# Accumulating transfers in DRAM in place of two additions on engines, in one step of an encoder layer

## The chip, the cores and the metric

The kernel runs on one core of a Trainium2 chip. The metric is the device time of one execution in microseconds; the kernel before takes 2776.52 us (median of three runs).

## What is computed

One layer of an encoder for two groups of requests that share the weights: a prompt of 2048 tokens and eight samples of 16 tokens, 17 tiles of 128 tokens in all. After a mixer (attention and a matrix memory) comes the part that matters here, a feed-forward net with a convolution and a norm on its output:

```python
def conv_ffn(h, buf, w_up, w_conv, b_conv, w_down):
    S = h.shape[1]
    u = h @ w_up
    ext = jnp.concatenate([buf.astype(u.dtype), u], axis=1)
    y = b_conv
    for j in range(CONV_W):
        y = y + ext[:, j:j + S] * w_conv[j]
    gate, up = jnp.split(y, 2, axis=-1)
    out = (jax.nn.gelu(gate, approximate=True) * up) @ w_down
    return out, ext[:, S:]
...
    ffn, new_buf = conv_ffn(rms_norm(x, norm_g[2]), conv_buf, w_up, w_conv, b_conv, w_down)
    x = x + rms_norm(ffn, norm_g[3])
```

The model width is 1024, the inner width 2816 (22 slices of 128, for gate and up each).

## The kernel before

The net works on three blocks of tokens: block 0 and block 1 with six tiles each, block 2 with four prompt tiles and the sample tile. Each block has an up projection and then a down projection. Everything is float32, made of three matmuls on split values: every weight and every activation is split into a high part (ACT, L1309) and a low part (DVE, L1310) before it is multiplied, in the helper `split`.

**Up projection.** A loop over the 22 slices f (I call one of its turns a round; `ORDERS` takes f and f + 11 in turn in blocks 1 and 2). A round makes the gate and the up slice by a scheme of seven half-size products, 7 x 12 = 84 matmuls, 384 wide in block 1 and 320 in block 2. DVE adds the products' results into two tiles, `uu` and `ug` (L1483, L1619, L1621, L1642); three such tiles are handed out in turn. `conv` lets GpSimd (POOL) copy two columns of the neighbouring block into the tile (L1494, L1497) and two columns out of it (L1499, L1498), then ACT (L1502, L1506) and DVE (L1503, L1504) do the convolution, and DVE multiplies gate and up into `g` (L1652, L1655). In block 1 that product stands in the tile `y`.

**Activation sums.** In blocks 1 and 2 the down projection is a product by seven as well. For that `store_a` keeps, per pair of slices k and k + 11, the parts A11, A12, A22 and four sums in DRAM (the tensors `ad`). In the pair's second round DVE makes S3, S1, S2 and S4 (L1595) into four of the pool's six spare tiles, and POOL stores them (L1597). S1 is A21 + A22, where A21 is the second part of the pair's first tile and A22 the second part of its second tile. In block 2 the sample tile's columns are stored on their own (L1577).

**Delayed norms.** The down projection leaves the un-normed output halves f0 and f1 of each tile of blocks 0 and 1 in DRAM, and `unfinished` keeps the tile's scale. While the next block's up projection runs, one unit per round (12 in block 1, 12 in block 2, from the fourth round on) finishes half a tile: SP loads f (L1427) and the residual x (L1428) from DRAM into two spare tiles, DVE scales f by the row's scale and the norm's weights (L1431), POOL adds x (L1432) and POOL issues the store of the result into the output (L1433). The loads and the scaling keep their written place among the other instructions of SP and DVE (`keep_in_program_order`); all else is ordered by a scheduler that plans with a model of the engines, so a change in one step can move others.

SP issues the loads of weights and activations, POOL the stores of this part. The transfers that one engine issues start in its order, and an instruction that waits holds up all that stands behind it on that engine.

Of the kernel before, what the change touches and what calls it, by code (L numbers as in the profile page):

```python
# [13 lines left out]
ALU = mybir.AluOpType  # L14
# [35 lines left out]
def hymba_step(ctx: ExitStack, tc: tile.TileContext, I: dict, O: dict):  # L50
    nc = tc.nc
# [17 lines left out]
    def spare_tile(name):  # L69
        return spare.tile([P, 512], F32, tag="k", name=name)  # L70

    def dt_(shape, name):
        return dram.tile(shape, F32, tag=name, name=name)
# [22 lines left out]
    def norm_row(i):  # L96
        t = const.tile([P, D], F32, tag="grow", name=f"norm_row{i}")
        nc.sync.dma_start(t, I["norm_g"][i:i + 1, :].broadcast_to([P, D]))
        return t


    def mm3(out, ah, al, bh, bl, start, stop, onto=False):
# [20 lines left out]
    ad = {(b, what): dt_([P, NK, 256 if b == 2 and what in ("A22", "S2", "S3") else 384], f"ad{b}_{what}")  # L123
          for b in FAST for what in ("A11", "A12", "A22", "S1", "S2", "S3", "S4")}
# [3 lines left out]
    x2d = [dt_([P, D], f"x2d{t}") for t in range(17)]  # L128
# [933 lines left out]
    def row(name):  # L1062
        return ffn.p3.tile([P, D], F32, tag="yq", name=name, bufs=4)
# [181 lines left out]
    for n_, (half, gi) in enumerate(seq):  # L1245
        wh, wl, _ = pend
# [154 lines left out]
    def out_rows(t):  # L1401
        return O["y_sample"] if t == SAMPLE else O["y_prompt"][t * P:(t + 1) * P, :]
# [20 lines left out]
    def later(t, rs):  # L1423

        def unit(half):
            v, x, c = spare_tile(f"f{half}{t}"), spare_tile(f"x{half}{t}"), half * 512
            tc.keep_in_program_order(nc.sync.dma_start(v, (f0d, f1d)[half][t]))  # L1427
            tc.keep_in_program_order(nc.sync.dma_start(x, x2d[t][:, c:c + 512]))  # L1428
            yield 0.0, 0.0
            tc.keep_in_program_order(  # L1430
                nc.vector.scalar_tensor_tensor(v, v, rs, g3[:, c:c + 512], op0=ALU.mult, op1=ALU.mult))  # L1431
            nc.gpsimd.tensor_tensor(v, v, x, op=ALU.add)  # L1432
            nc.gpsimd.dma_start(out_rows(t)[:, c:c + 512], v)  # L1433
            yield 0.0, 1.0

        return [unit(half) for half in range(2)]

    def delayed(units):

        for u in units:  # L1440
            next(u)
            yield
            next(u)

    ph.close()
    p4 = ffn.p4 = ctx.enter_context(tc.tile_pool(name="p4", bufs=1, side="right", reuse_waits="tile"))
# [3 lines left out]
    g3 = norm_row(3)  # L1450
# [15 lines left out]
    for b, tiles in enumerate(FBLOCKS):  # L1466
# [108 lines left out]
        def store_a(f, gt):  # L1575
            put = lambda what, k, src: nc.gpsimd.dma_start(ad[b, what][:, k, :], src)
            own = lambda what, k, src: nc.gpsimd.dma_start(ad[b, what][:, k, 256:384], src)  # L1577
            w = 256 if last else 384
            k = f % NK
            if f < NK:  # L1580
                put("A11", f, gt[:, 0:384])
                if last:
                    own("S1", k, gt[:, 256:384])
                held[f] = gt
                return
            put("A12", k, gt[:, 0:384])
            put("A22", k, gt[:, 384:384 + w])
            if last:
                own("S4", k, gt[:, 256:384])
            gt1 = held.pop(k)  # L1590
            a11, a21, a12, a22 = gt1[:, 0:w], gt1[:, 384:384 + w], gt[:, 0:w], gt[:, 384:384 + w]
            s3, s1, s2, s4 = [spare_tile(f"s{x}_{b}_{k}")[:, :w] for x in (3, 1, 2, 4)]
            for o, x, y, op in ((s3, a11, a21, ALU.subtract), (s1, a21, a22, ALU.add), (s2, a22, s3, ALU.subtract),
                                (s4, a12, s2, ALU.subtract)):
                nc.vector.tensor_tensor(o, x, y, op=op)  # L1595
            for what, src in (("S3", s3), ("S1", s1), ("S2", s2), ("S4", s4)):
                nc.gpsimd.dma_start(ad[b, what][:, k, 0:w], src)  # L1597

        done = delayed([u for t, rs in unfinished for u in later(t, rs)])
        unfinished = []  # L1600
        for fi, f in enumerate(ORDERS[b]):
            w = pend.pop(0)
# [11 lines left out]
            e, c = ec[:, 0:512], ec[:, 512:1024]  # L1614
# [10 lines left out]
            w = pend.pop(0)  # L1625
# [21 lines left out]
            gt = yg if fast and not last else row(f"g{nm}")  # L1647
# [9 lines left out]
            if fast:  # L1657
                store_a(f, gt)
            else:
                nc.gpsimd.dma_start(gd[b][f][:, :nt * P], gt[:, :nt * P])  # L1660
# [147 lines left out]
        for dh in range(2):  # L1808
# [59 lines left out]
            for j in order:  # L1868
                if dh == 0:
                    half, ssq = out[j]  # L1870
# [3 lines left out]
                else:  # L1874
                    half, ssq = out[j]
# [3 lines left out]
                    rs = p3.tile([P, 1], F32, tag=f"drs{j}", name=f"drs{tiles[j]}", bufs=2)  # L1879
# [104 lines left out]
```

## Time and profile before

| | us |
|---|---|
| median of three runs | 2776.52 |
| fastest and slowest of the three | 2768.33, 2780.66 |
| the profiled execution | 2780.55 |
| its span | 2778.8 |
| up projection of block 1 | about 1862 to 2165 of the span |
| up projection of block 2 | about 2352 to 2640 of the span |

PE is TensorE (PEld its weight loads), DVE VectorE, ACT ScalarE, POOL GpSimd, SP SyncE; a q behind a name means the engine's queue, which waits and issues. A row of instructions names line, engine, operation, output <- inputs and shape; behind the bar stand busy time, mean time of one in ns, and the idle time before them with what ended it. A row of a stretch gives its start and end, its length, then busy time and number of instructions per engine, PE's granted clock (1.00 is full), the share of time that the 16 DMA engines moved data, and GB/s. A row of transfers gives how many, KB each, and the median us from issue to landing.

### The profile page before, as it was taken

How to read it: one execution, taken by the hardware profiler on the slowest of the kernel's cores; microseconds unless marked ns; L12 is line 12 of the kernel's file. 1: busy time of each engine (PE TensorE's matmuls, PEld its weight loads, DVE VectorE, ACT ScalarE, POOL GpSimd, SP SyncE). 2: the span in 40 equal slices, each digit the busy share in tenths (PEclk: the TensorE clock that was granted, in tenths of full speed). 3: DMA queues.
4: the chain of work that ended last, by engine and by line, in shares of the span. 5: the costliest groups of instructions: out<-in, count | busy, mean ns of one | idle time of the engine just before them, and what ended most of it. 6: DMA issues, size and time to landing. Idle time of an engine off the chain costs nothing.

```text
span 2778.8 us, 47788 instructions
## 1 busy us (share of the span) xinstructions
PE 2700.5 (97%) x16422; PEld 2525.1 (91%) x16422; DVE 1971.7 (71%) x3637; ACT 1439.6 (52%) x2918; POOL 658.6 (24%) x1249
## 2 busy tenths in 40 slices
PE   7999999999999999999999999999999999999998
PEld 7899999998899998878999998789999778989976
DVE  5244455645546668766989987668998866999966
ACT  4355555634346666543555455445455665545554
POOL 1000010211100002335433322123442112555301
PEclk9999999999999999999999999999999999999999
DMA  5534355556564456345645559866775766777775
GB/s 182 157 116 139 105 164 168 163 152 211 156 184 141 136 169 196 107 163 195 230 153 188 167 183 329 301 224 198 225 225 170 250 223 231 216 236 231 233 268 183
DMA packets 322850, 532.52 MB, mean 192 GB/s; under 512 B 59650, under 2 KB 156638, under 8 KB 322478
## 3 DMA queue, kind: packets, MB, share of 16 engines
q1 hardware_dynamic: 251838, 400.11, 46.6%
q0 software_dynamic: 25840, 83.98, 7.9%
q10 hardware_dynamic: 44928, 45.37, 5.0%
q8 instruction: 129, 2.11, 0.3%
q14 instruction: 115, 0.94, 0.1%
HBM read 383.28 MB, written 149.18 MB: 192 GB/s over the span
## 4 chain that ended last, share of the span: by engine, by line
PE 49%; DVE 5%; DMA 3%; issue 2%; ACT 1%; POOL 1%; SPq 0%; DVEq 0%; POOLq 0%; ACTq 0%
PE uec L104 5%; PE uec L105 5%; PE uec L106 5%; PE dn L106 4%; PE dn L105 3%; PE dn L104 3%; PE ua L106 3%; PE ua L105 3%; PE ua L104 3%; PE wo L106 2%; PE wo L104 2%; PE wo L105 2%; PE dnm L105 1%; PE dnm L106 1%; PE dnm L104 1%
## 5 line engine op out<-in xcount | busy, mean ns | idle before, releaser
L104 PE MATMUL uec<-B,wuh 128*128 128x384 f32 (+1 forms) x720 | 237.8, 331 | 11.8 <-DVE uu L1642 10.7
L105 PE MATMUL uec<-B,wuh 128*128 128x384 f32 (+1 forms) x720 | 236.5, 328 | 0.0
L106 PE MATMUL uec<-B,wul 128*128 128x384 f32 (+1 forms) x720 | 234.8, 328 | 0.0
L1309 ACT CAST wuh<-wu 128x512 fp32r<-128x512 f32 x255 | 141.4, 618 | 112.4 <-PE uec L105 105.4
L1310 DVE TENSOR_TENSOR wul<-wu,wuh 128x512 fp32r<-128x512 f32 x255 | 170.4, 703 | 4.0 <-DMA x2d<-mx 2.8
L405 DVE CUSTOM_DVE_ANT_0 tmp<-s,nb 128x640 f32<-128x640 f32 (+4 forms) x128 | 94.4, 738 | 95.6 <-PE s L395 94.2
L104 PE MATMUL vo<-wi_h,hT 128*128 128x256 f32 x544 | 155.2, 285 | 0.8 <-DVE mt L211 0.6
L106 PE MATMUL vo<-wi_h,hT 128*128 128x256 f32 x544 | 155.6, 286 | 0.0
L105 PE MATMUL vo<-wi_l,hT 128*128 128x256 f32 x544 | 154.8, 285 | 0.0
L104 PEld LDWEIGHTS uec<-B,wuh 128*128 128x128 f32 x720 | 136.2, 189 | 15.3 <-DVE uu L1642 12.4
L104 PE MATMUL qk<-hT,wi_h 128*128 128x384 f32 (+1 forms) x384 | 130.3, 339 | 7.4 <-ACT qk_st L236 4.1
L105 PEld LDWEIGHTS uec<-B,wuh 128*128 128x128 f32 x720 | 136.4, 189 | 0.2
L106 PEld LDWEIGHTS uec<-B,wul 128*128 128x128 f32 x720 | 136.2, 189 | 0.0
L1506 ACT ACTIVATE y<-y 128x768 f32<-128x768 f32 (+1 forms) x66 | 53.8, 815 | 155.5 <-DVE y L1504 155.5
L418 DVE TENSOR_TENSOR ptl<-pt,pth 128x640 fp32r<-128x640 f32 (+4 forms) x128 | 93.7, 738 | 56.5 <-ACT pth L417 55.5
L406 ACT ACTIVATE tmp<-tmp,mn 128x640 f32<-128x640 f32 (+4 forms) x128 | 97.6, 762 | 64.2 <-DVE mn L405 62.4
L1310 DVE TENSOR_TENSOR wdl<-wdr,wdh 128x512 fp32r<-128x512 f32 x198 | 124.9, 686 | 7.0 <-ACT wdh L1309 6.8
L105 PE MATMUL qk<-hT,wi_h 128*128 128x384 f32 (+1 forms) x384 | 128.9, 336 | 0.0
L106 PE MATMUL qk<-hT,wi_l 128*128 128x384 f32 (+1 forms) x384 | 128.5, 335 | 0.0
L1310 DVE TENSOR_TENSOR al<-ar,ah 128x768 fp32r<-128x768 f32 (+2 forms) x94 | 71.1, 765 | 80.9 <-ACT ah L1309 80.7
L105 PE MATMUL qb<-hT,wi_h 128*128 128x384 f32 (+1 forms) x384 | 127.9, 333 | 0.0
L106 PE MATMUL qb<-hT,wi_l 128*128 128x384 f32 (+1 forms) x384 | 127.2, 331 | 0.0
(443 smaller groups left out, 9443.9 us busy)
## 6 DMA issues: line engine op xcount, KB each, us to landing
wu<-in_w_up SPq DMA_DIRECT2D x220, 256.0 KB, 4.4
wu<-wsd SPq DMA_DIRECT2D x176, 256.0 KB, 4.1
wdr<-in_w_down SPq DMA_DIRECT2D x110, 256.0 KB, 5.8
wi_raw<-in_w_in SPq DMA_DIRECT2D x52, 512.0 KB, 4.0
wsd<-ws POOLq DMA_DIRECT2D x88, 256.0 KB, 3.7
wdr<-wtd SPq DMA_DIRECT2D x88, 256.0 KB, 4.8
gr<-gd SPq DMA_DIRECT2D x39, 384.0 KB, 5.9
kraw<-kTd SPq DMA_DIRECT2D x112, 128.0 KB, 3.2
```

The lines of the kernel that those rows point to most:

```text
L104: nc.tensor.matmul(out, ah, bh, start=start, stop=False, skip_group_check=onto)
L105: nc.tensor.matmul(out, ah, bl, start=False, stop=False, skip_group_check=onto)
L106: nc.tensor.matmul(out, al, bh, start=False, stop=stop, skip_group_check=onto)
L405: nc.vector.tensor_tensor_reduce(o_, s_, b_, 1.0, 3e38, ALU.add, ALU.min, accum_out=mn)
L406: nc.scalar.activation(tmp[:, :n], tmp[:, :n], AF.Exp, bias=mn, scale=-1.0, accum_out=rsum[:, i % 4, hh:hh + 1])
L418: nc.vector.tensor_tensor(s.ptl[:, sl, qc], ptv, s.pth[:, sl, qc], op=ALU.subtract)
L1309: nc.scalar.copy(h, r)
L1310: nc.vector.tensor_tensor(l, r, h, op=ALU.subtract)
L1506: nc.scalar.activation(y[:, :ln], y[:, :ln], AF.Gelu_apprx_tanh)
```

## The change

A delayed unit no longer loads x and no longer adds it on POOL. Once DVE has scaled f, POOL issues a transfer that adds the tile onto x in DRAM, where x lies (`x2d`), and one that copies the sum from there to the output. In the code the copy of a unit is written one unit later, behind the next unit's accumulation. A unit takes one spare tile in place of two.

S1 is no longer made by DVE: POOL stores A21 as S1 in the pair's first round and adds A22 onto it in DRAM by an accumulating transfer in the second. A pair takes three spare tiles in place of four, and issues one transfer more.

```diff
@@ -1423,24 +1423,25 @@
     def later(t, rs):
 
         def unit(half):
-            v, x, c = spare_tile(f"f{half}{t}"), spare_tile(f"x{half}{t}"), half * 512
+            v, c = spare_tile(f"f{half}{t}"), slice(half * 512, half * 512 + 512)
             tc.keep_in_program_order(nc.sync.dma_start(v, (f0d, f1d)[half][t]))
-            tc.keep_in_program_order(nc.sync.dma_start(x, x2d[t][:, c:c + 512]))
             yield 0.0, 0.0
             tc.keep_in_program_order(
-                nc.vector.scalar_tensor_tensor(v, v, rs, g3[:, c:c + 512], op0=ALU.mult, op1=ALU.mult))
-            nc.gpsimd.tensor_tensor(v, v, x, op=ALU.add)
-            nc.gpsimd.dma_start(out_rows(t)[:, c:c + 512], v)
-            yield 0.0, 1.0
+                nc.vector.scalar_tensor_tensor(v, v, rs, g3[:, c], op0=ALU.mult, op1=ALU.mult))
+            nc.gpsimd.dma_start(x2d[t][:, c], v, accum_op=ALU.add)
+            yield 0.0, 0.7
+            nc.gpsimd.dma_start(out_rows(t)[:, c], x2d[t][:, c])
+            yield 0.0, 0.0
 
         return [unit(half) for half in range(2)]
 
     def delayed(units):
 
-        for u in units:
-            next(u)
+        for u, old in zip(units + [iter([])], [iter([])] + units):
+            next(u, None)
             yield
-            next(u)
+            next(u, None)
+            next(old, None)
 
     ph.close()
     p4 = ffn.p4 = ctx.enter_context(tc.tile_pool(name="p4", bufs=1, side="right", reuse_waits="tile"))
@@ -1579,21 +1580,22 @@
             k = f % NK
             if f < NK:
                 put("A11", f, gt[:, 0:384])
+                nc.gpsimd.dma_start(ad[b, "S1"][:, k, 0:w], gt[:, 384:384 + w])
                 if last:
                     own("S1", k, gt[:, 256:384])
                 held[f] = gt
                 return
             put("A12", k, gt[:, 0:384])
             put("A22", k, gt[:, 384:384 + w])
+            nc.gpsimd.dma_start(ad[b, "S1"][:, k, 0:w], gt[:, 384:384 + w], accum_op=ALU.add)
             if last:
                 own("S4", k, gt[:, 256:384])
             gt1 = held.pop(k)
             a11, a21, a12, a22 = gt1[:, 0:w], gt1[:, 384:384 + w], gt[:, 0:w], gt[:, 384:384 + w]
-            s3, s1, s2, s4 = [spare_tile(f"s{x}_{b}_{k}")[:, :w] for x in (3, 1, 2, 4)]
-            for o, x, y, op in ((s3, a11, a21, ALU.subtract), (s1, a21, a22, ALU.add), (s2, a22, s3, ALU.subtract),
-                                (s4, a12, s2, ALU.subtract)):
-                nc.vector.tensor_tensor(o, x, y, op=op)
-            for what, src in (("S3", s3), ("S1", s1), ("S2", s2), ("S4", s4)):
+            s3, s2, s4 = [spare_tile(f"s{x}_{b}_{k}")[:, :w] for x in (3, 2, 4)]
+            for o, x, y in ((s3, a11, a21), (s2, a22, s3), (s4, a12, s2)):
+                nc.vector.tensor_tensor(o, x, y, op=ALU.subtract)
+            for what, src in (("S3", s3), ("S2", s2), ("S4", s4)):
                 nc.gpsimd.dma_start(ad[b, what][:, k, 0:w], src)
 
         done = delayed([u for t, rs in unfinished for u in later(t, rs)])
```

The order on POOL around a unit, in block 2's up projection. Before, with `f_27653` the scaled half of a tile and `x_27654` its residual, `halo` and `sext` the columns kept between blocks, `uu` and `ug` the convolution's tiles:

```order
L1499 COPY halo<-ug_14_27734 128x2
L1498 COPY sext<-ug_14_27734 128x16
L1432 TENSOR_TENSOR f_27653<-f_27653,x_27654 128x512
L1433 DMA out_y_prompt<-f_27653 128x512
L1494 COPY uu_15_28059<-halo 128x2
L1497 COPY uu_15_28059<-sext 128x8x2
L1499 COPY halo<-ug_4_27911 128x2
L1498 COPY sext<-ug_4_27911 128x16
```

In the changed kernel the same place on POOL, where `x2d_288` is the residual's tile in DRAM (the lines of `conv` are one further on):

```order
L1500 COPY halo<-ug_14_27686 128x2
L1499 COPY sext<-ug_14_27686 128x16
L1431 DMA x2d_288<-f_27607 128x512
L1433 DMA out_y_prompt<-x2d_288 128x512
L1495 COPY uu_15_28006<-halo 128x2
L1498 COPY uu_15_28006<-sext 128x8x2
L1500 COPY halo<-ug_4_27859 128x2
L1499 COPY sext<-ug_4_27859 128x16
```

The scheduler put the copy to the output straight behind the accumulation that it waits for, ahead of the convolution's column copies. In block 2 six of the twelve units stand so; in the other six, two, four, one, two, four and two of the column copies come in between, 15 in all.

On DVE the rows of a pair's second round in block 2 (slices 2 and 13), before:

```order
L1642 TENSOR_TENSOR uu_3_27550<-x_2_3_27497,uec_3_27495 128x320
L1652 TENSOR_TENSOR g_13_27448<-y_13_0_27443,y_13_1_27435 128x2x256
L1655 TENSOR_TENSOR g_13_27448<-y_13_0_27443,y_13_1_27435 128x128
L1621 TENSOR_TENSOR x_2_14_27662<-x_2_14_27661,uec_14_27659 128x320
L1595 TENSOR_TENSOR s_2_2_27455<-g_2_27284,g_13_27448 128x256
L1595 TENSOR_TENSOR s_2_2_27456<-g_13_27448,s_2_2_27454 128x256
L1503 SCALAR_TENSOR_TENSOR y_3_1_27614<-uu_3_27550,wcv,y_3_1_27614 128x656
L1595 TENSOR_TENSOR s_2_2_27457<-g_13_27448,s_2_2_27456 128x256
```

and in the changed kernel:

```order
L1644 TENSOR_TENSOR uu_3_27503<-x_2_3_27450,uec_3_27448 128x320
L1654 TENSOR_TENSOR g_13_27405<-y_13_0_27400,y_13_1_27392 128x2x256
L1657 TENSOR_TENSOR g_13_27405<-y_13_0_27400,y_13_1_27392 128x128
L1623 TENSOR_TENSOR x_2_14_27614<-x_2_14_27613,uec_14_27611 128x320
L1597 TENSOR_TENSOR s_2_2_27413<-g_13_27405,s_2_2_27412 128x256
L1504 SCALAR_TENSOR_TENSOR y_3_1_27567<-uu_3_27503,wcv,y_3_1_27567 128x656
L1597 TENSOR_TENSOR s_2_2_27414<-g_13_27405,s_2_2_27413 128x256
```

The sum of the two tiles g_2 and g_13, which is S1, is gone; the rest of this piece stands in its old order.

## The prediction

> **What bounds the kernel now.** I read the page's first part, then busy times by stage, then what PE and DVE waited for in the one stage that loses time, then groups and single instructions there.
>
> ```profile
> PE 2700.5 (97%) x16422; PEld 2525.1 (91%) x16422; DVE 1971.7 (71%) x3637; ACT 1439.6 (52%) x2918; POOL 658.6 (24%) x1249
> ```
>
> PE is busy for 97% of the span, so at most 78 us could be won anywhere. The stages from the up projection of block 1 on, where the change acts:
>
> ```profile
> core 0: us, PE busy (x) PEld busy (x) DVE busy (x) ACT busy (x) POOL busy (x), PEclk, DMA share, GB/s
> 1862.00:2165.00 303.00, 302.28 (x1735) 301.96 (x1735) 275.12 (x406) 154.25 (x252) 112.05 (x179) 1.00 0.63 201
> 2165.00:2360.00 195.00, 191.76 (x900) 157.65 (x899) 135.21 (x210) 118.80 (x222) 29.90 (x59) 1.00 0.73 239
> 2360.00:2400.00 40.00, 40.00 (x275) 40.00 (x274) 37.22 (x77) 24.14 (x42) 17.56 (x38) 1.00 0.64 201
> 2400.00:2560.00 160.00, 149.88 (x988) 148.09 (x987) 151.59 (x296) 80.52 (x139) 94.57 (x171) 0.97 0.74 236
> 2560.00:2620.00 60.00, 60.00 (x411) 60.00 (x410) 55.91 (x118) 33.92 (x59) 26.40 (x62) 1.00 0.60 191
> ```
>
> Row one is block 1's up projection, with 12 delayed units: PE idles 0.7 of 303 us, so nothing is to be won there. Rows three to five are block 2's. Before its delayed units (2360 to 2400) and behind them (2560 to 2620) PE never idles. While the 12 units run (2400 to 2560), it does. At the pace of the fifth row (411 matmuls in 60 us, 6.85 per us) the 988 matmuls would take 144.2 us; they took 160. **The stretch loses 15.8 us**: 10.1 us of idle PE (160 less 149.88), and 5.7 us of slow matmuls. I call one value of f a round, 84 matmuls (7 products of 12): 11.8 rounds of 12.26 us at full pace.
>
> ```profile
> PE uec L104 <- DVE uu L1642: 9.7, 4, 4.2
> ```
>
> PE's idle time there is four waits for DVE. DVE was busy 151.59 us over work that PE needs 144.2 us for: 105%. Behind the units it is 55.91 of 60, 93%. So in this stretch alone DVE sets the pace. The longest wait, on the chain:
>
> ```profile
> 2463.80 6.03 DMA f<-f1d
> ...
> 2475.80 0.64 PE uec L104
> 2476.43 0.27 PE uec L105
> ```
>
> After it matmuls start every 0.27 us in place of 0.146 (60 over 411): the slow part.
>
> **The change part by part.** POOL's add of the residual goes, 24 times. Its price is paid by DVE as well:
>
> ```profile
> 2525.10 1.93 DVE L1503 SCALAR_TENSOR_TENSOR y<-ug,wcv,y 128x656 f32<-128x656 f32 x1
> ...
> 2527.35 0.89 DVE L1504 SCALAR_TENSOR_TENSOR y<-ug,wcv,y 128x656 f32<-128x656 f32 x1
> ```
> ```profile
> 2524.66 1.67 POOL L1432 TENSOR_TENSOR f<-f,x 128x512 f32<-128x512 f32 x1 [0.69 <-DVE f L1431]
> ```
>
> The DVE instruction that lies under the add takes 1.93 us, its like a moment later 0.89. For all adds, the groups of DVE with the units (2400 to 2556):
>
> ```profile
> L1310 DVE TENSOR_TENSOR wul<-wu,wuh 128x512 fp32r<-128x512 f32 x52 | 38.4, 768 | 0.0
> L1310 DVE TENSOR_TENSOR wu<-wu,wu 128x512 fp32r<-128x512 f32 x28 | 20.4, 744 | 0.0
> L1503 DVE SCALAR_TENSOR_TENSOR y<-ug,wcv,y 128x656 f32<-128x656 f32 x12 | 15.4, 1279 | 0.0
> L1504 DVE SCALAR_TENSOR_TENSOR y<-ug,wcv,y 128x656 f32<-128x656 f32 x12 | 11.7, 977 | 0.0
> ...
> L1431 DVE SCALAR_TENSOR_TENSOR f<-f,drs,norm_row 128x512 f32<-128x512 f32 x12 | 8.9, 744 | 1.7 <-DMA f<-f1d 1.7
> ...
> L1595 DVE TENSOR_TENSOR s<-g,g 128x256 f32<-128x256 f32 x6 | 2.5, 415 | 0.0
> ```
>
> and without (2562 to 2620):
>
> ```profile
> L1310 DVE TENSOR_TENSOR wul<-wu,wuh 128x512 fp32r<-128x512 f32 x24 | 15.4, 684 | 0.0
> L1310 DVE TENSOR_TENSOR wu<-wu,wu 128x512 fp32r<-128x512 f32 x8 | 5.3, 685 | 0.0
> L1504 DVE SCALAR_TENSOR_TENSOR y<-ug,wcv,y 128x656 f32<-128x656 f32 x5 | 4.5, 896 | 0.0
> L1503 DVE SCALAR_TENSOR_TENSOR y<-ug,wcv,y 128x656 f32<-128x656 f32 x5 | 4.5, 893 | 0.0
> ```
>
> The means differ by 84, 59, 386 and 81 ns: 52, 28, 12 and 12 times, 4.4 + 1.7 + 4.6 + 1.0 = 11.7 us of DVE, about 1 us per add. The S1 add (the row of L1595 with two g) goes too: 6 by 0.415 = 2.5 us. DVE's work in the stretch falls by 14.2 to 137.4 us: **95% of 144.2**. The number of its other instructions stays, and nearly all of their order.
>
> What is late next? At 93% PE lost nothing, at 105% 15.8 us. On the line between, 95.3% still loses 0.18 of it, 2.8 us. DVE's own wait for loads of f (1.7 us, the row of L1431) stays beside it. So 4.5 of the 15.8 us stay and **11.3 us go**.
>
> Three edits cost nothing that counts. SP no longer issues the 24 loads of x, and a unit draws one spare tile in place of two, a pair of rounds three in place of four. DMA: the accumulation's read takes the place of x's, and the copy reads 256 KB again, S1 about half of that per round: 12 times 0.38 MB, 4.6 MB, or 14 us at the stretch's 319 GB/s (236 over its share 0.74). That raises the share from 0.74 to about 0.83 and has the weight loads' lead as cover. Uncovered, a load that lands 1 us later would cost as much per round: 12 us.
>
> The edit that can cost is **POOL's new wait**. The copy to the output is issued from POOL and waits until the accumulation has landed; behind it wait the copies of the convolution's two columns (L1494 to L1499) and the stores of g.
>
> ```profile
> 2400.00:2556.00 156.00, 145.88 (x971) 144.09 (x969) 148.82 (x288) 78.89 (x137) 92.67 (x167) 0.98 0.74 236
> ```
> ```profile
> L1432 POOL TENSOR_TENSOR f<-f,x 128x512 f32<-128x512 f32 x12 | 19.7, 1646 | 11.6 <-DVE f L1431 8.5 <-DVE wul L1310 3.1
> ...
> L1433 POOL DMA_DIRECT2D out_y_prompt<-f x12 | 6.7, 559 | 2.7 <-POOL f L1432 2.4 <-POOL halo L1499 0.3
> ...
> L1494 POOL COPY ug<-halo 128x2 f32<-128x2 f32 x11 | 5.7, 519 | 2.3 <-DVE y L1504 1.8
> ```
>
> POOL is occupied for 92.67 us in 971/84 = 11.6 rounds, its DMA issues included. Without the adds that is 6.3 us per round; the accumulation's issue adds 0.56 and half an S1 issue 0.28: 7.1. A round leaves 5.1 us for the wait, and what the order puts between accumulation and copy (15 copies in 12 units, 0.5 us each, 0.6 per unit) runs under it: **5.7 us**. How long does an accumulation take to land? No row shows one. The nearest:
>
> ```profile
> x<-x2d SPq DMA_DIRECT2D x24, 256.0 KB, 4.4
> out_y_prompt<-f POOLq DMA_DIRECT2D x24, 256.0 KB, 3.9
> ```
>
> A plain store of the same tile from POOL's queue is the lower bound, 3.9 us; that store behind a full read of the destination the upper, 3.9 + 4.4 = 8.3. I take 5, near the store, since it is the same queue and bytes and the two reads can run side by side. Then a round of POOL takes 7.1 + 5 - 0.6 = 11.5 us, under 12.26. A late POOL has slack besides:
>
> ```profile
> 2523.44 0.53 POOL L1498 COPY sext<-uu 128x16 f32<-128x16 f32 x1
> ```
> ```profile
> 2532.93 0.41 ACT L1640 COPY ug<-ua 128x320 f32<-128x320 f32 x1
> ```
>
> This save ends at 2523.97, and the write of the tile's next user, three u tiles on, starts at 2532.93: 9.0 us. In block 1 the wait fits at either bound:
>
> ```profile
> 1905.00:2080.00 175.00, 175.00 (x1006) 175.00 (x1004) 164.33 (x236) 88.37 (x144) 80.34 (x113) 1.00 0.69 219
> ```
> ```profile
> L1432 POOL TENSOR_TENSOR f<-f,x 128x512 f32<-128x512 f32 x12 | 30.1, 2512 | 12.3 <-DVE f L1431 12.3
> ```
>
> (80.34 - 30.1)/12 = 4.2, with issues 5.0, with 8.3 us of wait 13.3 of 14.6 us per unit.
>
> On that landing time the Trainium skill has a formula (DMA: Bandwidth & Descriptors, Anatomy of one DMA): about 2.0 us plus the bytes over 436 GB/s for a transfer issued from GpSimd, 2.6 us for this tile. The trace's stores take 3.9, so the measurement decides; by the formula POOL would need 9.1 us a round and never be late, and the sum would stay the same.
>
> **Sum.** The profiled execution took 2780.55 us (span 2778.8). Less 11.3, 2769. The median of the three runs is 4.0 lower, which gives 2765. I say **2767 us**.
>
> **Rivals.** *POOL takes DVE's place (slower).* At 8.3 us a round of POOL is 14.8 us, 2.5 over 12.26; 12 units make it 30 us late, less 9 of slack 21 us on PE, in place of the 15.8 lost now: 5 us slower, 2786, and 2792 if PE pays slow matmuls again (5.7). It decides from a landing of (15.8 + 9)/12 + 5.7 = 7.8 us. For it: the order puts the copy right behind the accumulation in half of the units. Against: 3.9 us for the plain store. The Trainium skill (Collectives: The Full Stack, The bandwidth ceiling) says that an adding transfer reads two sources with two read descriptors per chunk and moves at half rate; no run here shows it. Twice 3.9 would be 7.8, this rival's threshold.
>
> *The load of f is the next bound.* Loads of f stay pinned in SP's order, every second one just ahead of its use. A DVE that is 1.2 us per unit earlier (14.2 over 12) may only meet them earlier and wait out what it gained: 14 us of waits, DVE is at 105% again, and the time stays at about 2778. For it: the 6.03 us ahead of the longest wait. Against: 1.7 us is all that DVE waited for f now.
>
> *Only the S1 part works.* If DVE is slowed as much by POOL's added DMA issues as by the add, 2.5 us are left: 2774 to 2778. Against it: between 2562 and 2620 POOL issues stores and DVE's means are the low ones.
>
> **How the numbers follow.** Forecast (2757 to 2773) 0.58; f load or S1 alone (2773 to 2781) 0.22; POOL bound 0.20. Low end: all of the 15.8 us off the median, 2760.7, and a few us at the stage's end, where the last five S1 adds go (2 us): 2757. High end: the slower rival with slow matmuls, 2793. About one in ten lies outside. 0.5% (13.9 us) is about what a measurement of this kernel tells from no change: below 2762.6 lies a third of the forecast, and little else, 0.21; above 2790.4 the worse part of the slower rival and an accumulation longer than 8.3 us, 0.15; between them 0.64.
>
> **What would show it.** Right: DVE's y and wul groups at 893 and 684 ns with units running; PE idle under 4 us between 2400 and 2550; accumulations that land in 4 to 6.5 us. Wrong: PE or DVE waiting for POOL's halo copies; POOL's wait on x2d above 7 us; DVE waiting over 10 us for f.

## The result and the profile after

The changed kernel takes 2769.12 us (median of 15 runs, 2765.79 to 2776.61), the kernel before 2776.97 us (15 runs beside them, 2768.33 to 2780.66). The ratio is **0.9975, 95% interval 0.9966 to 0.9984**: 7.9 us less. This is under the 0.5% (13.9 us) that the prediction takes as needed to tell a change from none; the interval leaves out 1 all the same, so the changed kernel is faster, by little. The forecast was 2767 us. A second set of 11 runs (e9 below) gave 2772.26 us and 0.9984 (0.997 to 0.9997).

The total of the forecast holds; several of its terms don't, and the stretch that was to bring the gain brings only part of it. One thing ahead has to be set right: by their first and last matmuls the up projections before run from 1845.1 to 2175.6 of the span (block 1) and from 2338.5 to 2634.0 (block 2). The stretches of the prediction lie inside them, but for the one from 2165 to 2360, which holds the end of one and the start of the other.

The page's first part, after:

```profile
PE 2693.8 (97%) x16422; PEld 2520.4 (91%) x16422; DVE 1943.2 (70%) x3615; ACT 1438.5 (52%) x2918; POOL 654.3 (24%) x1271
```

DVE has 22 instructions and 28.5 us less. Busy times by stage, after (PE, PEld, DVE, ACT, POOL, then granted clock, DMA share, GB/s):

```profile
1862.00:2165.00 303.00, 302.47 (x1727) 300.95 (x1726) 261.85 (x396) 153.50 (x248) 101.11 (x189) 1.00 0.72 210
2165.00:2360.00 195.00, 193.34 (x934) 161.36 (x932) 136.72 (x218) 123.42 (x230) 37.56 (x66) 1.00 0.73 239
2360.00:2400.00 40.00, 40.00 (x276) 40.00 (x275) 35.90 (x75) 21.43 (x37) 18.32 (x42) 1.00 0.75 218
2400.00:2560.00 160.00, 154.06 (x1020) 151.84 (x1020) 144.34 (x299) 84.82 (x149) 92.58 (x185) 0.98 0.82 243
2560.00:2620.00 60.00, 60.00 (x390) 58.28 (x388) 55.04 (x116) 33.44 (x59) 27.95 (x60) 1.00 0.75 250
```

Row four is the stretch of the forecast. Its 1020 matmuls need 148.9 us at 6.85 per us, so 11.1 us are lost where before lost 15.8. Idle PE fell from 10.1 to 5.9 us, and DVE stands at 144.34 of 148.9 us of PE's work, 97%. Row one lost nothing before and loses nothing now, also with the copies' waits in it. DVE's groups with the units (2400 to 2556):

```profile
L1310 DVE TENSOR_TENSOR wul<-wu,wuh 128x512 fp32r<-128x512 f32 x56 | 36.3, 684 | 0.0
L1310 DVE TENSOR_TENSOR wu<-wu,wu 128x512 fp32r<-128x512 f32 x28 | 18.5, 684 | 0.0
L1504 DVE SCALAR_TENSOR_TENSOR y<-uu,wcv,y 128x656 f32<-128x656 f32 x12 | 10.8, 898 | 5.0 <-ACT y L1503 4.9
...
L1505 DVE SCALAR_TENSOR_TENSOR y<-ug,wcv,y 128x656 f32<-128x656 f32 x12 | 10.7, 894 | 0.0
L1504 DVE SCALAR_TENSOR_TENSOR y<-ug,wcv,y 128x656 f32<-128x656 f32 x12 | 10.7, 894 | 0.0
...
L1430 DVE SCALAR_TENSOR_TENSOR f<-f,drs,norm_row 128x512 f32<-128x512 f32 x11 | 8.2, 746 | 1.2 <-DMA f<-f1d 1.2
```

The drag is gone as forecast: 768, 744, 1279 and 977 ns became 684, 684, 894 and 894. The wait for f is 1.2 us, so the rival with the load of f fell. What grew is DVE's waiting for ACT's y: 7.2 us in 9 waits between 2330 and 2645, before 2.9 in 3. PE's waits, and the new ones of ACT and POOL (2350 to 2640: total, times, longest):

```profile
PE uec L104 <- DVE uu L1644: 3.9, 4, 1.5
PE dn L104 <- ACT ah L1309: 2.5, 2, 2.2
PE ua L104 <- ACT wuh L1309: 1.6, 1, 1.6
```
```profile
ACT y L1503 <- DMA ad_S<-g: 11.7, 4, 7.2
```
```profile
POOL out_y_prompt L1433 <- DMA x2d<-f: 30.4, 6, 6.2
```

PE waits 3.9 us for DVE in place of 9.7. The 1.6 us for ACT's cast `wuh` are new. (The 2.5 us for `ah` belong to the last down projection, behind this up projection; before shows 0.9 there.) ACT waits for a *store* (ad_S<-g) to land, because the tile of y that it writes is taken from the row tiles of g, and they are free only when POOL's stores from them are through. What holds the stores up is seen in the longest round (the 14th), first in POOL's own order, then on ACT and PE:

```profile
2485.82 0.96 POOL L1431 DMA_DIRECT2D x2d<-f  x1
2491.85 0.56 POOL L1433 DMA_DIRECT2D out_y_prompt<-x2d  x1 [5.07 <-DVE y L1504]
...
2495.95 0.55 POOL L1583 DMA_DIRECT2D ad_S<-g  x1
2496.49 0.54 POOL L1577 DMA_DIRECT2D ad_A<-g  x1
2497.02 0.54 POOL L1578 DMA_DIRECT2D ad_S<-g  x1
```
```profile
2502.46 0.93 ACT L1503 ACTIVATE y<-uu,wcv 128x656 f32<-128x656 f32 x1 [7.19 <-DMA ad_S<-g]
2503.30 2.16 ACT L1309 CAST wuh<-wu 128x512 fp32r<-128x512 f32 x4
```
```profile
2503.96 0.42 PE L104 MATMUL ua<-B,wuh 128*128 128x320 f32 x1 [1.63 <-ACT wuh L1309]
```

POOL stands 5.07 us at the copy. The row names DVE, but what the copy needs is the accumulation, which was issued 6 us earlier. Behind the copy come column copies, and only then the stores of g, the last at 2497.02. ACT stands for 7.19 us until that store has landed, 5.4 us after its issue; its y starts, the casts of the weights come behind it, and PE has sat idle for 1.63 us when the first of them is there. The store waited for (L1578) is the one of the sample tile's columns; S1's store (L1583) is ahead of it on the queue. The landing times, by issue groups (KB each, median us) and for the accumulation's line:

```profile
x2d<-f POOLq DMA_DIRECT2D x24, 256.0 KB, 6.0
out_y_prompt<-x2d POOLq DMA_DIRECT2D x24, 256.0 KB, 4.1
```
```profile
DMA to landing us min/median/max: 4.7/6.0/7.7
```

6.0 us, against 5 taken and bounds of 3.9 and 8.3. On POOL the accumulation's instruction takes 1.03 us (median 0.88) in place of the 0.56 of a plain one:

```profile
L1431 POOL DMA_DIRECT2D x2d<-f x11 | 11.4, 1033 | 3.4 <-DVE f L1430 3.4
...
L1433 POOL DMA_DIRECT2D out_y_prompt<-x2d x11 | 6.1, 558 | 54.0 <-DMA x2d<-f 30.4 <-ACT ug L1642 6.3 <-DVE g L1657 6.0
```

The Trainium skill (Collectives: The Full Stack, The bandwidth ceiling) has the adding transfers of a reduce-scatter at about half the rate of plain copies, because the add reads two sources. It says so of the bandwidth of such a ring of cores, not of the landing of one tile; twice the plain store's 3.9 would be 7.8 us. Here the landing took 1.5 times as long as the plain store's, 6.0.

### The profile page after: what moved, and what is told of

Read it like the earlier page. It is cut to its first block, busy times and chain, and to the rows that moved or that the text cites. A ratio compares the mean times of both kernels' runs of the same rounds, so it can differ in the third digit from the quotient of the medians.

```text
span 2767.0 us, 47747 instructions
## 1 busy us (share of the span) xinstructions
PE 2693.8 (97%) x16422; PEld 2520.4 (91%) x16422; DVE 1943.2 (70%) x3615; ACT 1438.5 (52%) x2918; POOL 654.3 (24%) x1271
## 4 chain that ended last, share of the span: by engine, by line
PE 53%; DVE 3%; DMA 2%; issue 1%; POOL 1%; ACT 1%; DVEq 0%; POOLq 0%; SPq 0%; ACTq 0%
PE uec L104 6%; PE uec L105 6%; PE uec L106 6%; PE dn L106 4%; PE dn L105 4%; PE dn L104 4%; PE ua L106 3%; PE ua L105 3%; PE ua L104 3%; PE wo L106 2%; PE wo L104 2%; PE wo L105 2%; PE dnm L106 2%; PE dnm L105 2%; PE dnm L104 2%
## 5 line engine op out<-in xcount | busy, mean ns | idle before, releaser
L105 PE MATMUL qb<-hT,wi_h 128*128 128x384 f32 (+1 forms) x384 | 127.9, 333 | 0.0
L104 PE MATMUL qb<-hT,wi_h 128*128 128x384 f32 (+1 forms) x384 | 127.1, 331 | 0.0
```

Of the source, the lines that this page charges most:

```text
L104: nc.tensor.matmul(out, ah, bh, start=start, stop=False, skip_group_check=onto)
L105: nc.tensor.matmul(out, ah, bl, start=False, stop=False, skip_group_check=onto)
```

## The experiments

My theory after the result: POOL's add drags on DVE, and its removal is the gain; POOL's wait for the accumulation gives part of it back through the stores of g. Rivals: the gain is S1's alone; the wait costs nothing and DVE simply needs more room; the loss that the sum began from was too large.

Ratios are to the kernel before on the same chip. For each profiled execution I also give block 2's up projection from its first to its last matmul, and its *long rounds*: the starts of every 84th matmul are 12.3 us apart in block 2, except in a few rounds, mostly the 8th, 11th, 14th and 17th. That column adds up what the rounds take over 12.3 us, without the first and the last. One kernel's executions differ in it by 1 to 5 us, so a single one proves little; groups of them do. The last two columns are what PE waited for DVE's last sum into uu in block 2, and how long the granted clock was 0.50 in its up projection.

| kernel | median us | ratio (95%) | up projection, us | long rounds over 12.3, us | PE waits for uu, us | clock at 0.50, us |
|---|---|---|---|---|---|---|
| before | 2776.97 | | 295.6 | 15.6 | 9.7 | 10.2 |
| e12: before, second profile | | | 290.6 | 10.6 | 7.5 | 3.4 |
| after | 2769.12 | 0.9975 (0.9966 to 0.9984) | 290.3 | 10.9 | 3.9 | 6.8 |
| e9: after again | 2772.26 | 0.9984 (0.997 to 0.9997) | 291.8 | 12.3 | 4.4 | 3.4 |
| e1: norm part only | 2770.65 | 0.9975 (0.9965 to 0.9985) | 289.1 | 9.1 | 5.9 | 3.4 |
| e2: S1 part only | 2774.0 | 0.9982 (0.9972 to 0.9992) | 293.8 | 14.3 | 8.8 | 10.2 |
| e3: copy later | 2769.53 | 0.9969 (0.996 to 0.9979) | 285.3 | 5.8 | 4.5 | 0 |
| e10: copy later, again | 2767.36 | 0.9966 (0.9953 to 0.9979) | 287.1 | 7.7 | 4.7 | 3.4 |
| e11: copy later, norm only | 2770.26 | 0.9975 (0.9966 to 0.9984) | 289.4 | 9.4 | 6.2 | 3.4 |
| e4: copy issued by SP | 2783.28 | 1.0018 (1.0004 to 1.0032) | 300.6 | 21.1 | 13.7 | 13.7 |
| e5: before without the add | 2770.59 | 0.9975 (0.9962 to 0.9988) | 287.3 | 7.3 | 5.6 | 0 |
| e6: straight onto the output | 2774.2 | 0.9987 (0.9977 to 0.9998) | 285.2 | 5.8 | 4.4 | 0 |
| e7: e3 and an idle add | 2772.76 | 0.9985 (0.9974 to 0.9995) | 291.9 | 12.4 | 8.0 | 6.8 |
| e8: accumulated twice | 2793.19 | 1.0056 (1.0039 to 1.0074) | 309.8 | 30.3 | 5.5 | 23.9 |

The waits for uu sort the kernels: 7.5 to 9.7 us in the four profiles with an add on POOL in each unit (before, e12, e2, e7), 3.9 to 6.2 in nine without it; e4 stands apart for another reason. The clock blurs the long rounds, and partly by chance (last section). At 0.50 a matmul starts every 0.27 us in place of 0.146, so I estimate 1.6 us of long rounds per 3.4 us at 0.50. Without these, the four with an add have 9.0 to 10.9 us, the three with no add and S1 on DVE (e1, e5, e11) 7.3 to 7.8, the three with no add, S1 accumulated and no wait on POOL (e3, e10, e6) 5.8 to 6.1, and the changed kernel 7.8 and 10.7.

**e1, e2: the two parts alone.** e1 is the changed kernel with S1 made on DVE again:

```diff
-                nc.gpsimd.dma_start(ad[b, "S1"][:, k, 0:w], gt[:, 384:384 + w])
...
-            nc.gpsimd.dma_start(ad[b, "S1"][:, k, 0:w], gt[:, 384:384 + w], accum_op=ALU.add)
...
+            for o, x, y, op in ((s3, a11, a21, ALU.subtract), (s1, a21, a22, ALU.add), (s2, a22, s3, ALU.subtract),
+                                (s4, a12, s2, ALU.subtract)):
```

> Only the delayed units are changed; S1 is made by DVE and stored as before. If the gain is the end of GpSimd's adds lying on DVE (about 1 us of DVE per add, 12 in block 2's stretch, against 2.5 us for S1), most of it stays: 2769 to 2773 us, DVE's groups at their low means, and GpSimd's waits for the accumulation as in the changed kernel. If S1 carries the gain, this is at 2775 or more.

e2 is the kernel before with only the S1 lines of the change.

> Only S1 is changed; the delayed units load x and add it on GpSimd as before. By the first theory 2.5 us of DVE go in a stretch where DVE lacks 7 us and GpSimd issues one more transfer of 0.9 us per pair: 2774 to 2777 us, y and wul still at the high means. If S1 carries the gain: 2769 to 2771.

Measured: 0.9975 for the norm part, 0.9982 for S1. The norm part alone gains 7.3 us, S1 alone 4.0. e2 leaves PE's waits for uu at 8.8 us and wul at 804 ns (e1: 681), so the rival "only S1" fell. The two sum to 11.3 us, and together they gave 7.9 (5.4 in e9); each of these gains is uncertain by some 3 us, so that the parts don't add up is likely and not shown. What S1 brings lies mostly outside of the stretch: from block 1's last up matmul to block 2's first one there are 162.9, 163.5, 163.2, 162.6 and 162.7 us in the five executions with S1 on DVE (before, e12, e1, e5, e11), and 159.1 to 161.0 in the nine with S1 accumulated. The sum had no term for it (the low end of the range counts 2 us for the last S1 adds), and what shortens this part is not shown. In the stretch S1 seems to hurt together with the norm part: 9.1 us of long rounds in e1, 10.9 and 12.3 in the changed kernel. e3, e10 and e11 tell more of that.

**e3: the copy later.** The change with both DMAs of a unit pinned in their order, so that on POOL each copy stands behind the next unit's accumulation, and its own has long landed:

```diff
-            nc.gpsimd.dma_start(x2d[t][:, c], v, accum_op=ALU.add)
+            tc.keep_in_program_order(nc.gpsimd.dma_start(x2d[t][:, c], v, accum_op=ALU.add))
             yield 0.0, 0.7
-            nc.gpsimd.dma_start(out_rows(t)[:, c], x2d[t][:, c])
+            tc.keep_in_program_order(nc.gpsimd.dma_start(out_rows(t)[:, c], x2d[t][:, c]))
```

> The changed kernel with both transfers of a unit kept in written order on GpSimd, so that the copy stands behind the next unit's accumulation and its own has long landed. If GpSimd's wait (6 us per unit) gives part of the gain back, by late stores of g and so late rows for ACT and DVE: 2762 to 2767 us, almost no wait on x2d, and block 2's up projection under 288 us. If what is left is DMA traffic or the loads of f: 2768 to 2771, as the changed kernel.

Measured: 2769.53 us (0.9969), which is the range expected if DMA traffic or the loads of f are what is left, and not to be told from the changed kernel's 0.9975. The profiled stretch still shows what was meant:

```profile
2400.00:2560.00 160.00, 155.52 (x1055) 154.25 (x1054) 147.52 (x306) 86.41 (x150) 94.05 (x190) 1.00 0.87 250
```
```profile
PE uec L104 <- DVE uu L1644: 4.5, 4, 2.1
PE dn L104 <- ACT ah L1309: 2.5, 1, 2.5
```

1055 matmuls in 160 us, 35 more than in the changed kernel, and 6.0 us lost in place of 11.1. ACT no longer waits for a store of g, nor POOL for an accumulation. This execution lost time elsewhere: from the last up matmul to PE's last one it took 141.1 us, before 135.5 and 135.6. A load for the last down projection had not come (ACT waits 3.9 us for ar<-ad_A, PE 2.5 for ACT's ah), and behind that the granted clock was 0.50 for 6.8 us:

```profile
2620.00:2660.00 40.00, 36.53 (x145) 28.15 (x144) 22.41 (x38) 19.81 (x36) 4.41 (x9) 0.91 0.79 265
```

The changed kernel shows the same, weaker (139.2 us, with 3.4 at 0.50; in e9 137.8, with none). e10, the same kernel as e3, needs 137.1 us, with none: what e3 lost to the clock here is this execution's.

**e4: the copy on SP.** The same delay, but issued by SP:

```diff
-            nc.gpsimd.dma_start(out_rows(t)[:, c], x2d[t][:, c])
+            tc.keep_in_program_order(nc.sync.dma_start(out_rows(t)[:, c], x2d[t][:, c]))
```

> The changed kernel with the copy issued from SP, kept in written order one unit later. GpSimd loses the wait and 0.56 us of issue per unit. If GpSimd's wait gives part of the gain back: 2761 to 2766 us. If DMA traffic or the loads of f are what is left: 2768 to 2771. If SP's queue is what matters, the copies hold up weight loads: over 2771.

Measured: 2783.28 us, slower than before, the third of the cases expected. What DVE and PE wait for:

```profile
DVE f L1430 <- DMA f<-f1d: 18.5, 5, 5.2
```
```profile
PE uec L104 <- DVE uu L1644: 13.7, 4, 6.0
```

On SP's queue the copies stand among the loads. SP stands 37.5 us at them in 12 waits (2400 to 2560) until the accumulation has landed, and the load of f comes late: 18.5 us of waits on DVE against 1.2 in the changed kernel. So the rival "load of f" is a real bound, but not one that this change touches.

**e5: no add at all.** The kernel before without POOL's add:

```diff
-            nc.gpsimd.tensor_tensor(v, v, x, op=ALU.add)
```

> The kernel before without GpSimd's add in the delayed units: x is still loaded, f is scaled and stored, so the output rows of blocks 0 and 1 lack the residual. S1 stays on DVE, and nothing new waits. If the add's drag on DVE (11.7 us in block 2) is what the change removes: 2766 to 2770 us, y and wul at the low means. If the drag is not what delays PE: 2775 to 2779.

Measured: 2770.59 us, 0.9975, just above the range expected if the drag is what goes; 7.3 us of long rounds against 10.6 and 15.6. Taking the add away, and nothing else, gives as much as the whole norm part of the change (e1). DVE's groups, wul with the units and y:

```profile
L1310 DVE TENSOR_TENSOR wul<-wu,wuh 128x512 fp32r<-128x512 f32 x56 | 36.6, 684 | 0.0
L1503 DVE SCALAR_TENSOR_TENSOR y<-ug,wcv,y 128x656 f32<-128x656 f32 x13 | 11.6, 895 | 0.0
```

**e6: straight onto the output.** The residual of tiles 0 to 11 is stored into the output as well when the mixer makes it, and the accumulation goes there; copy and wait are gone:

```diff
             nc.sync.dma_start(x2d[t], xr)
+            if t < 12:
+                nc.sync.dma_start(O["y_prompt"][t * P:(t + 1) * P, :], xr)
...
-            nc.gpsimd.dma_start(x2d[t][:, c], v, accum_op=ALU.add)
+            nc.gpsimd.dma_start(out_rows(t)[:, c], v, accum_op=ALU.add)
             yield 0.0, 0.7
-            nc.gpsimd.dma_start(out_rows(t)[:, c], x2d[t][:, c])
-            yield 0.0, 0.0
```

> The changed kernel with the residual of tiles 0 to 11 stored into the output as well, in the mixer's stage, and the accumulation made there: no copy and no wait. If GpSimd's wait and the copies cost anything on top of the copy-later kernel: 2762 to 2767 us. If what is left is DVE alone: 2767 to 2770, as copy-later.

A miss: 2774.2 us, outside of what was expected, although its up projection is the shortest of all (285.2 us). The profiled execution took 2769.53 us, the lowest of this kernel's 12 runs, so it can't show where the others lose. Whether the 12 added stores of 512 KB cost it was not tried apart.

**e7: the drag back.** e3 with an add of the same size on POOL ahead of each accumulation, whose result nobody reads:

```diff
+            nc.gpsimd.tensor_tensor(junk, v, v, op=ALU.add)
             tc.keep_in_program_order(nc.gpsimd.dma_start(x2d[t][:, c], v, accum_op=ALU.add))
```

> The copy-later kernel with a GpSimd add of the same size put back ahead of each accumulation, into a tile that nobody reads. If it is the add's drag on DVE that the change removed: about 1 us of DVE per unit comes back, 2774 to 2778 us, y and wul at the high means. If the gain came from the loads of x or the spare tiles: it stays at 2768 to 2771.

Measured: 2772.76 us (0.9985), between the two ranges expected. Its gain over before is 5.1 us, that of e3 and e10 8.4 and 10.3; the intervals still overlap a little, so the times alone don't settle it. The trace does: 12.4 us of long rounds against 5.8 and 7.7, and PE's waits for uu at 8.0 us against 4.5 and 4.7. DVE with the units:

```profile
L1310 DVE TENSOR_TENSOR wul<-wu,wuh 128x512 fp32r<-128x512 f32 x55 | 40.6, 773 | 0.0
L1505 DVE SCALAR_TENSOR_TENSOR y<-ug,wcv,y 128x656 f32<-128x656 f32 x11 | 11.4, 1033 | 0.0
L1506 DVE SCALAR_TENSOR_TENSOR y<-ug,wcv,y 128x656 f32<-128x656 f32 x12 | 11.1, 923 | 0.0
```

An add that gives nothing to anyone makes DVE's means rise again, 684 to 773 ns on wul: it is the add's being there, not its place in a chain of dependences. It costs 5 to 7 us of long rounds, 2 to 3 of them slow matmuls by the estimate above. Nor is it POOL's time: in before nobody waits for POOL in this stretch, in e7 ACT does for 0.3 us.

**e8: two landings in a row.** The changed kernel with the accumulation made twice; the second waits for the first:

```diff
             nc.gpsimd.dma_start(x2d[t][:, c], v, accum_op=ALU.add)
+            nc.gpsimd.dma_start(x2d[t][:, c], v, accum_op=ALU.add)
```

> The changed kernel with the accumulation of a unit done twice, the second behind the first's landing (the output rows of blocks 0 and 1 get the norm's result added twice). GpSimd waits two landings per unit, 12 us, and needs 17 to 20 us for a round of 12.3 us in block 2 and of 14.6 in block 1. If GpSimd then sets the pace: 2830 to 2900 us. If its waits are covered: under 2775.

Measured: 2793.19 us (1.0056), slower, but by far less than expected: 15.3 us over before, for 24 added landings of about 6 us. (The profiled execution is the slowest of its six, 2797.03 us.) The two DMAs that wait on POOL, in block 2 (2400 to 2580):

```profile
L1432 POOL DMA_DIRECT2D x2d<-f x12 | 10.4, 865 | 55.7 <-DMA x2d<-f 38.5 <-DVE y L1505 7.3 <-ACT wuh L1309 5.2
L1434 POOL DMA_DIRECT2D out_y_prompt<-x2d x12 | 7.2, 600 | 27.0 <-DMA x2d<-f 17.2 <-DVE y L1505 4.4 <-DVE wu L1310 4.0
```
```profile
2400.00:2580.00 180.00, 163.03 (x1025) 158.40 (x1024) 144.54 (x299) 83.20 (x145) 94.32 (x194) 0.93 0.86 235
```

POOL stood 82.7 us ahead of these two, 6.9 per unit, not two full landings of 12: what the order puts between them ran meanwhile. With the 94.32 us of busy time POOL was taken for 177 of 180 us. Here **POOL is the bound**; in the changed kernel it is taken for 146.6 of 160 (92.58 and 54.0). The waits of ACT and PE name the path:

```profile
ACT y L1504 <- DMA ad_S<-g: 20.8, 3, 9.5
```
```profile
PE ua L104 <- ACT wuh L1309: 8.3, 3, 4.0
PE uec L104 <- DVE uu L1645: 5.5, 4, 2.2
```

It is the path of the longest round above, wider: the stores of g land late, ACT's y waits for the row tile, ACT's casts of the weights (wuh) stand behind it, and PE waits for those. Beside it stands the path that the prediction had priced: ACT's y waits 17.1 us for POOL's column copies (9.1, 4.6 and 3.4), which it never does in the changed kernel.

**e9, e10, e11: the order of the copy, on one chip.** e9 is the changed kernel, e10 the kernel of e3, e11 that with S1 on DVE.

> The changed kernel once more, beside the next two on one chip. 2768 to 2772 us. If the pair of GpSimd's wait and rows of g held by the S1 accumulation costs time, it is 2 us or more slower than copy-later beside it, and ACT's waits for stores of g (11.7 us in the profile of the changed kernel, none in copy-later) come back; if that wait is an accident of one execution, they don't.

> The copy-later kernel on the same chip: 2766 to 2770 us, block 2's up projection at about 285 us, no wait of ACT for stores of g. Same as the changed kernel within 1 us if GpSimd's wait is covered after all.

> Copy-later with S1 made by DVE as before. DVE has 2.5 us more to do in block 2's stretch, GpSimd one transfer less per pair. If only DVE's load counts now: up projection of block 2 at 286 to 288 us and 1 to 4 us slower than copy-later in all, 2769 to 2773. If GpSimd's and the DMA's work counts: as fast or faster, 2765 to 2768.

Measured side by side: 2772.26, 2767.36 and 2770.26 us, the first just above its range, the others inside. The copy later is 4.9 us better in the medians here, 12.3 to 7.7 us in the long rounds; the intervals of the two ratios (0.997 to 0.9997 and 0.9953 to 0.9979) still overlap, and in the first pair (after and e3, not run side by side) there was no difference in the medians. In e9 ACT again waits for the store of g (14.1 us in 3 waits, the longest 7.0), in e10 and e11 never. With the copy later, S1's part adds 2.9 us of gain in the medians (e11 to e10), with intervals that overlap; e10's up projection was 2 us longer than expected, e11's 1.4 above its range. The best version that ran is this one, 0.9966 and 0.9969 of before.

**e12: before, a second profile.**

> The kernel before, unchanged, profiled a second time: the first profiled execution took 2780.55 us, 3.6 over its median. If its block-2 up projection was a usual one, this one lasts 294 to 297 us again from the first to the last up matmul (295.6 before), with its four long rounds 11 to 16 us over 12.3 in all. If it was an unlucky one, the sum began from too large a loss: then 289 to 293 us, and the change's own gain there is under 3 us.

Measured: 290.6 us, and this stretch:

```profile
2400.00:2560.00 160.00, 152.28 (x1022) 150.96 (x1022) 155.39 (x303) 83.60 (x144) 101.39 (x176) 0.99 0.74 241
```
```profile
PE uec L104 <- DVE uu L1642: 7.5, 4, 2.4
```

1022 matmuls, so 10.8 us lost in place of 15.8, with DVE as busy as ever (155.39 of 149.2, 104%). The longest wait for DVE is 2.4 us, not 4.2, and the 11th round 14.3 us in place of 19.0, and the clock was at 0.50 for 3.4 us, not 10.2. By what was expected, the execution on which the sum was made was an unlucky one; two executions don't say what is usual.

## Why the prediction was right, and where it was not

*DVE is the bound while the units run, and POOL's add is why: right, and shown.* e5 takes only the add away and gains 7.3 us; e7 puts only an add back, and 5.1 us are left of the gains of e3 and e10, 8.4 and 10.3. PE's waits for uu go with the add in every profile but e4's (the table). The means of DVE's groups fell to those of the undisturbed stretch.

On that the Trainium skill has a rule (SBUF — State Buffer, Who interferes with whom): a VectorE instruction with two inputs in SBUF contends with a GpSimd instruction that reads SBUF. The traces agree: the rows wul and y read two SBUF tiles, and with an add on POOL wul took 765 to 804 ns (before, e12, e2, e7), without it 681 to 684 (after, e1, e3, e5, e6, e11). POOL's accumulating and plain DMA issues, of which this rule does not speak, left them at 684 and 894 ns.

*DVE's relief of 14.2 us: nearly right.* At like numbers of matmuls, 1022 in e12 and 1020 after, DVE was busy 155.39 and 144.34 us: 11.0 less. In shares, 104% became 97%, not 95%.

*11.3 of 15.8 us go: the step that failed,* in three places that the runs tell apart. Where the sum had 11.3 us, block 2's up projection became 2 us shorter (293.1 us on the mean of the two profiles before, 291.0 of the two after).
- **The 15.8.** e12 lost 10.8 us with the same kernel. I had one execution, 3.6 us over its median, and took its loss in one stretch as the kernel's. By the two executions about 13 us is the size.
- **The line from 105% to 93%.** With DVE relieved and nobody held up (e3, e10), 6.0 and 7.7 us are still lost where the line left 2.8 and a wait 1.7. The loss is not spread over the stretch: it stands in four rounds, three apart, in which PE waits for DVE's uu (4.5 us in e3). A mean share can't see that.
- **POOL's wait at nothing.** The landing was 6.0, not 5, and the issue 1.03, not 0.56, so that my sum for POOL's round is 7.6 + 6.0 - 0.6 = 13.0 us, over the 12.26 (it waited 54.0/11 = 4.9 per unit, so more ran under the landing than I counted). The slack that I named, 9 us on the u tiles, did hold: neither PE nor DVE ever waited for a halo copy. But I priced only that cover. The stores of g stand behind the wait too, I wrote so, and they hold the row tiles that ACT needs next; by the runs it takes S1's transfers from the same rows besides, since e1, with 24.3 us of the same waits on POOL and S1 on DVE, shows none of it. How S1 does this is not shown: the store that ACT waits for is the sample tile's own, which e1 has too. Together they cost 3 to 7 us of long rounds (10.9 and 12.3 against 7.7 and 5.8), 2 to 5 without the estimate for the clock.

So in the stretch about 13 us of loss became 11 to 12, and would be 6 to 8 with the copy later.

*Two terms that the sum lacked.* From block 1's to block 2's up projection the kernels with S1 accumulated need about 3 us less (163.2 before on the mean, 159.9 after). At its end the changed kernel needs about 3 us more (138.5 against 135.6): ACT waits there for ar<-ad_A, 5.4 and 6.7 us against 3.3 and 2.6 before. I take it that an up projection that ends sooner meets loads that come no sooner; no run tried that apart. These two are about even. The medians show 7.9 and 5.4 us; from block 0's first up matmul to PE's last one the profiled executions show 1446.7 and 1443.1 us before and 1442.2 twice after, 2.7 on the mean. The whole profiled executions differ by 7.1 us on the mean, and 4.1 of these lie ahead of block 0's first up matmul (1322.8 and 1320.7 us before, 1315.9 and 1319.5 after), where the change has no instruction. So the traces place 2.7 us of a gain of 5.4 to 7.9; the rest lies within what executions differ by, and I can't assign it.

*The total was right largely by luck:* too large a loss, less too large a relief, on a profiled time that was itself high by 3.6 us, and two terms that were missing and about cancel.

*The rivals.* "POOL takes DVE's place": not at one landing of 6.0 us (threshold 7.8); with two in a row it is what happens (e8, 1.0056). "Load of f": 1.2 us; it becomes true on SP's queue (e4). "Only S1": no (e1, e2). Of the signs I named, the means were right, the landing times were right in the median (6.0, up to 7.7), PE idle was not: 5.9 us in this stretch, where under 4 were to show.

## What to carry to other kernels

A transfer that adds in DRAM frees the compute engines, but its issuer pays in waiting when the result is copied on from the same queue: put that copy behind the next unit's work, and follow *everything* that stands behind the wait to the tiles it holds, stores first. And where a stretch loses time in a few bunches, take its loss from two executions, and look for the rounds in which it falls, before dividing busy time by a pace.

## What was not expected of the hardware

PE's clock makes small waits dear, and not in every execution. It is half of the reason why two executions of one kernel differ by 5.0 us in one stretch: 2.4 us are idle PE (10.1 in before, 7.7 in e12), 2.6 are slow matmuls (5.7 and 3.1). In e12, by single microseconds (PE busy is the first figure after the length, the clock the third from the end):

```profile
2431.00:2432.00 1.00, 0.00 (x0) 0.00 (x0) 1.00 (x3) 0.03 (x1) 0.02 (x1) 1.00 0.74 209
2432.00:2433.00 1.00, 0.10 (x1) 0.10 (x1) 1.00 (x3) 0.00 (x0) 0.00 (x0) 1.00 0.80 238
...
2435.00:2436.00 1.00, 1.00 (x6) 1.00 (x5) 1.00 (x3) 0.84 (x2) 1.00 (x3) 0.50 0.42 98
2436.00:2437.00 1.00, 1.00 (x5) 1.00 (x5) 1.00 (x3) 1.00 (x3) 0.93 (x2) 0.50 0.75 201
```

PE is idle for 1.94 us, and 1.3 us after it has work again the granted clock is 0.50 for 3.4 us: 5 or 6 matmuls touch a microsecond in place of 9, and they start every 0.27 us in place of 0.146. In the changed kernel 1.63 us of idle PE at 2502 were followed by 6.8 us at 0.50. But at the same wait the first profile of before shows as long an idle PE, 1.94 us, and no fall:

```profile
2432.00:2433.00 1.00, 0.00 (x0) 0.00 (x0) 1.00 (x3) 0.00 (x0) 0.00 (x0) 1.00 0.71 182
...
2435.00:2436.00 1.00, 1.00 (x9) 1.00 (x8) 1.00 (x3) 0.86 (x2) 1.00 (x3) 1.00 0.63 213
```

Over block 2's up projection in all 14 profiles, all seven idle stretches of PE of 2.99 us and more went with a fall to 0.50, during them or within 1 us behind them; of the 20 between 1.6 and 2.9 us 11 did, the fall at most 1.4 us behind; of the shorter ones none. The Trainium skill (TensorE: Matmul & The Clock Gate, Part 1) has the clock halved after at least one idle window of about 3.4 us, with windows that run freely. The length of the slow stretches, once or twice 3.4 us, agrees, and free windows would explain that one idle stretch is followed by a fall and its like is not; that 1.63 and 1.94 us of idling can be enough does not agree, and here the measurement decides.
